# A fused decoder layer on one core: the second group's values and queries become filler of the second heads

## The chip, the cores and the metric

The kernel runs on one core of a Trainium2 chip. The metric is the time of one execution on the device in microseconds (us). Engines are named as in the profile: PE multiplies matrices (PEld loads its weights), DVE, ACT and POOL work on vectors, SP issues most transfers. Each engine works through its own queue in order; a semaphore wait at the head of a queue holds all that stands behind it.

## The reference

One decoder layer in float32 on x (512 tokens of 2048), with a norm at the end. After a first norm one projection gives the queries, keys and values of two groups of heads; both outputs are normed, joined and projected back, and a gated feed-forward part follows.

```
h = rmsnorm(x, ln_mix); proj = h @ w_in
sb_q, sb_k, sb_v, sw_q, sw_k, sw_v = split(proj)
sb_o = stick_breaking_attention(sb_q, sb_k, sb_v)              # 16 heads
sw_o = sliding_window_sink_attention(sw_q, sw_k, sw_v, sinks)  # 16 query heads, 4 key heads, window 128
x = x + concat(rmsnorm(sb_o), rmsnorm(sw_o)) @ w_out
h = rmsnorm(x, ln_ffn); x = x + (silu(h @ w_gate) * (h @ w_up)) @ w_down
return rmsnorm(x, ln_final)
```

A sliding-window head subtracts slope times distance from its scores, takes the maximum with a learned sink, exponentiates, divides by the sum and multiplies with the values.

## The kernel before

Every float32 operand is held as a high part and the rest (names ending in hi and lo), and a product is three matmuls: hi by hi, lo by hi, hi by lo. A weights' slab is 512 KB: a transfer on SP (`raw`, three tiles), a rounding to the high part on ACT (`whi`, L219, two tiles), the rest on DVE (`wlo`, L220, two tiles), then 24 matmuls of 128x512 or 48 of 128x256 on PE.

The stages, by the time in the profile: 0 to 59 us load and transposes of x, the split of the normed h (`h_make`), and the first projection (`add_kq`); here `left_sums` prepares sums of h for the following stage and `x_squares` squares x for the norm. To 140 the values of the first heads. To 431 the sixteen stick-breaking heads, "the first heads". To 458 the rest of their filler. From 459 to 603 the sliding-window heads, "the second heads": four groups of queries with four blocks of 128 tokens each, sixteen jobs. To about 730 the rest of the output projection, then the feed-forward part to the end at 2009.

**Filler.** An attention head alone would leave PE idle, so the projections around it are cut into slabs and put into `queue`. `step` issues one piece of the slab at its front; `pull(ns)` issues pieces worth so many nanoseconds, `drain(mark)` all up to a mark. `step` also loads the two slabs that come next and splits one. In the first heads the queue holds 32 slabs of queries and keys for the heads to come, the second heads' keys (swk), group 2's queries, and three of the four slabs of the second heads' values (swv); `sb_mark` ends it. In the second heads it holds the last slab of values, group 3's queries and the sixteen slabs of outA, which is the output projection of the first heads' half, column block by column block (`add_outA(c)`, c from 0 to 3). Behind them is outB.

`banks` of add_outA runs when a column block's first piece is issued:

```
x2[c] = v8.tile([P, NT, 512], F32, tag="v8", name="x2")
dma(out=x2[c], in_=x2d[:, c * 512:(c + 1) * 512].rearrange("(t p) c -> p t c", p=P))
```

`dma` keeps SP's transfers in the order in which the program issues them. `v8` is a pool of four tiles of 1 MB; a new tile takes one whose last reader is done. In the second heads v8 holds kst[0], qst[0] and qst[1] (the stacked keys of groups 0 and 1, the queries of groups 0 and 1) and x2; kst[1], qst[2] and qst[3] lie in another pool (`act8`).

**A job of the second heads** is spread over three rounds: scores (L1061, L1062) into a PSUM bank; on DVE the distance term (L1076) and the maximum (L1080); on ACT four exponentials (L1090); the scaling by the sum (L1102 ACT, L1104 DVE); transposes on PE (L1112); their high part on ACT (`phi`) and rest on DVE (`plo`, L1116); the product with the values (L1125, L1126). Four PSUM banks (`z`) serve scores, transposes and products. Between them stand four pulls of `SWFILL`/4.

The order on each engine is not the order of the code: a scheduler arranges the instructions, and only those issued through `pV`, `pA`, `pG`, `pT` and `dma` keep their program order.

Of the kernel before, what the change touches and what calls it, by code (L numbers as in the profile page):

```python
# [16 lines left out]
P = 128  # L17
# [4 lines left out]
HD = 64  # L22
# [15 lines left out]
def tile_hymba(ctx: ExitStack, tc: tile.TileContext, x, ln_mix, w_in, sb_norm, swa_norm,  # L38
# [27 lines left out]
    def act8(name, dt=F32R):  # L66
        return act.tile([P, 4, 512], dt, tag="a8", name=name, bufs=8)
# [10 lines left out]
    def po():  # L78
        return bank("o", 2)
# [14 lines left out]
    def tmp(dt=F32, name="t"):  # L94
        return phase[1].tile([P, 512], dt, tag="t", name=name, bufs=phase[2])
# [227 lines left out]
    def h_make(kt):  # L323
        pb = pz()
        for t in range(NT):
            pT.transpose(out=pb[:, t * P:(t + 1) * P], in_=xs[kt, t], identity=ident)
            warm({(0, 0): 1, (0, 1): 1, (0, 2): 3, (1, 3): 3}.get((kt, t), 0))
        if kt % 4 == 0:
            h8[0], h8[1] = act8("hhi"), act8("hlo")
        h_hi[kt], h_lo[kt] = h8[0][:, kt % 4, :], h8[1][:, kt % 4, :]  # L330
        split_scaled(pb, gcol[:, kt:kt + 1], h_hi[kt], h_lo[kt])
        if kt % 4 == 0:
            h8s.append((h8[0], h8[1]))
        if kt > 1:
            while vsum:
                vsum.pop(0)()
        left_sums(kt, pb)

    def left_sums(kt, pb):
        g, j, gc = kt // 8, kt % 4, gcol[:, kt:kt + 1]  # L340
        if kt % 8 == 0:
            vs = [v8.tile([P, 4, 512], F32, tag="v8", name="vs") for _ in range(2)]
            for k, p in enumerate("5736"):
                vleft[g, p] = vs[k // 2][:, :, (k % 2) * 256:(k % 2) * 256 + 256]
        s1, s3, s4, s2 = (vleft[g, p][:, j, :] for p in "5736")
        a, b = pb[:, 0:256], pb[:, 256:512]

        def stt(out, x, y, op):
            V.scalar_tensor_tensor(out=out, in0=x, scalar=gc, in1=y, op0=ALU.mult, op1=op)

        if kt % 8 < 4:
            pG.tensor_tensor(out=s1, in0=f(h_hi[kt])[:, 256:512], in1=f(h_lo[kt])[:, 256:512], op=ALU.add)
            vsum.append(lambda: stt(s3, a, s1, ALU.subtract))
        else:
            vsum.append(lambda: (stt(s1, b, s1, ALU.add), stt(s2, b, s3, ALU.subtract), stt(s4, a, s2, ALU.subtract)))

    def x_squares(c):
        for t in range(NT):
            xt = xs["c", c, t]
            A.activation(out=xt, in_=xt, func=AF.Square, accum_out=ss1[:, t, c:c + 1])  # L360

    def rstd1_make():
        sst = sm.tile([P, NT], F32, tag="sst", name="sst")
# [42 lines left out]
    def add_feat(w, cols, get_banks, done, hfn=hT):  # L406
        bk = {}

        def one(c, j, s):
            def go(hi, lo):  # L410
                k = s * 4 + j
                xh, xl = hfn(k)
                wh, wl = hi[:, j, c * P:(c + 1) * P], lo[:, j, c * P:(c + 1) * P]
                o = bk["b"][c]
                mm(o, lhsT=wh, rhs=xh, start=(k == 0), stop=False)  # L415
                mm(o, lhsT=wh, rhs=xl, start=False, stop=False)  # L416
                mm(o, lhsT=wl, rhs=xh, start=False, stop=(k == KT - 1))  # L417
                if k == KT - 1:
                    done(c, o)
                return 648.0  # L420
            return go

        for s in range(4):
            if s in (0, 3):
                mms = [one(c, j, s) for c in range(2) for j in range(4)]
            else:
                mms = [one(c, j, s) for j in range(4) for c in range(2)]
            queue.append(dict(srcs=[w[s * 512:(s + 1) * 512, c0:c0 + cn] for c0, cn in cols], a=4, b=256,
                              mms=mms, pre=(lambda: bk.update(b=get_banks())) if s == 0 else None,
                              post=None, prep=None, big=None))  # L430
# [117 lines left out]
    vst = [None] * NT  # L548
    swv = [None]
    kq = [None]  # L550
    KTS = ((), (2, 3), (4, 5), (6, 7), (8, 9, 10), (11, 12, 13), (14, 15), ())

    def add_kq():
        bk = {}

        def one(c, j, s):
            def go(hi, lo):
                k = s * 2 + j
                xh, xl = h_hi[k], h_lo[k]
                wh, wl = hi[:, j, c * P:(c + 1) * P], lo[:, j, c * P:(c + 1) * P]  # L560
                o = bk["b"][c]
                mm(o, lhsT=wh, rhs=xh, start=(k == 0), stop=False)
                mm(o, lhsT=wh, rhs=xl, start=False, stop=False)
                mm(o, lhsT=wl, rhs=xh, start=False, stop=(k == KT - 1))
                if k == KT - 1:
                    if c == 0:
                        kq[0] = const.tile([P, 4, 512], F32, tag="swv", name="kq")
                    if c % 2:
                        A.activation(out=kq[0][:, c, :], in_=o, func=AF.Copy)
                    else:  # L570
                        V.tensor_copy(out=kq[0][:, c, :], in_=o)
                return 648.0
            return go

        def prep(s):
            for kt in KTS[s]:
                h_make(kt)
            for c in {3: (0, 1), 5: (2,), 6: (3,)}.get(s, ()):
                x_squares(c)

        for s in range(8):
            order = [(c, j) for c in range(4) for j in range(2)] if s == 7 else [(c, j) for j in range(2) for c in range(4)]
            rows = slice(s * 256, (s + 1) * 256)
            queue.append(dict(srcs=[win[rows, C_SWQ:C_SWQ + 512]], a=2, b=512, big=None,
                              mms=[one(c, j, s) for c, j in order], post=None,
                              pre=(lambda: bk.update(b=four(1))) if s == 0 else None, prep=lambda s=s: prep(s)))
# [97 lines left out]
    def q_evac(pb, dst):  # L684
        V.scalar_tensor_tensor(out=dst, in0=pb, scalar=QSCALE, in1=rs1["b"], op0=ALU.mult, op1=ALU.mult)
# [13 lines left out]
    def stack_one(src, r0, st):  # L699

        s64 = src[r0:r0 + HD]
        r1 = HD - r0
        A.activation(out=st[r0:r0 + HD], in_=s64, func=AF.Copy)
        V.tensor_tensor(out=st[r1:r1 + HD], in0=s64, in1=f(st)[r0:r0 + HD], op=ALU.subtract)
# [50 lines left out]
        vof(n + 2, "to_hp")  # L755

    drain_to(5, 3)
    while vsum:
        vsum.pop(0)()
    x_squares(4)  # L760
    open_phase("vp", 1, reuse_waits="tile")
    for n in range(-6, 0):
# [43 lines left out]
    drain_to(11, 0)  # L806
    oA = [o8.tile([P, 4, 512], F32, tag="o8", name="oA") for _ in range(2)]
    kqs = ExitStack()
    kq2 = kqs.enter_context(tc.tile_pool(name="kq2", bufs=1, side="right", reuse_waits="tile")).tile([P, 4, 512], F32, name="kq2")
    add_feat(win, [(C_SWK, 256)], two_m, lambda c, pb: k_evac(pb, kq2[:, c, :]))  # L810
    add_feat(win, [(C_SWQ + 512, 256)], two_m, lambda c, pb: q_evac(pb, kq2[:, 2 + c, :]))
    add_swv()
    swv_end = len(queue)
    sb_mark = swv_end - 1
    z3 = {}
    for name in ("sh3", "sl3", "wh3", "wl3"):
        z3[name] = sbt(F32R, name, 256)
# [168 lines left out]
    def stack_keys(c):  # L986
        for e in range(2):
            stack_two(kq2[:, c, :], e * HD, kst[c][:, 2 * e, :], kst[c][:, 2 * e + 1, :])

    def stack_queries(g, src):  # L990
        for c in range(2):
            for e in range(2):
                stack_one(src[:, c, :], e * HD, qst[g][:, c * 2 + e, :])

    kst[0], qst[0], qst[1] = (v8.tile([P, 4, 512], F32R, tag="v8", name=n) for n in ("kst", "qst", "qst"))
    stack_keys(0)
    stack_queries(0, kq[0][:, 0:2, :])

    def add_swq3():
        def done(c, pb):  # L1000
            qf = tmp(name="qf")
            q_evac(pb, qf)
            for e in range(2):
                stack_one(qf, e * HD, qst[3][:, c * 2 + e, :])

        def tiles():
            kst[1], qst[2], qst[3] = act8("kst"), act8("qst"), act8("qst")

        n = len(queue)
        add_feat(win, [(C_SWQ + 768, 256)], lambda: [po(), po()], done)  # L1010
        queue[n + 1]["post"] = tiles

    add_swq3()
    swq3_end = len(queue)


    mixA = [None] * 10
# [117 lines left out]
    blks = {}  # L1135
    jobs = [(g, blk) for g in range(4) for blk in range(NT)]
    NJ = len(jobs)
    SWFILL = 5200.0 * 1.0
    at(swa_scores, 0)
    stack_queries(1, kq[0][:, 2:4, :])  # L1140
    for j in range(NJ + 2):
        at(swa_exp, j)
        pull(SWFILL / 4)
        at(swa_tr, j - 1)
        pull(SWFILL / 4)
        if j == 2:
            drain(swv_end)
        if j == 5:
            drain(swq3_end - 2)
            stack_keys(1)  # L1150
        if j == 6:
            stack_queries(2, kq2[:, 2:4, :])
        if j == 10:
            drain(swq3_end)
        at(swa_av, j - 2)
        pull(SWFILL / 4)
        at(swa_norm, j)
        at(swa_scores, j + 1)
        pull(SWFILL / 4)
# [692 lines left out]
```

## Time and profile before

| what | value |
|---|---|
| median of 3 runs | 2009.11 us (2008.97 to 2009.53) |
| the profiled execution | 2010.75 us, its span 2009.0 us |
| mean granted clock of PE | 0.997 |
| PE busy | 1992.6 us (99%) |
| DVE, ACT, POOL busy | 1498.7, 1503.0, 1106.1 us |

A timeline row reads: start, duration, engine, line, operation, output<-inputs, shape, count; in brackets the idle time of the engine just before and what ended it. A duration of a matmul overlaps the next one, so starts are compared. A row of the waits reads: engine, tile and line that waited, what for, us in total, times, longest. Rows of `wlo` at L220, of `whi` at L219 and of transfers at L100 are those of a helper; the tile tells which.

### The profile page before, as it was taken

What the parts mean: (1) busy time and instruction counts of PE and PEld (TensorE: products, weight loads), DVE (VectorE), ACT (ScalarE), POOL (GpSimd) and SP (SyncE); (2) the same over time, 40 slices, a digit from 0 to 9 for tenths busy, and PEclk for the clock granted to TensorE, in tenths of its full rate; (3) what the DMA queues carried; (4) which work ended last, traced back from release to release, by engine and by line L of the source; (5) the groups of instructions that cost most, each with busy time, mean ns of one, the idle gap of its engine ahead of it and who ended that gap; (6) DMA issues with size and microseconds to landing.
All of it is one profiled execution on the core that took longest, in us unless ns stands there. A gap on an engine that the chain in (4) does not pass through costs nothing.

```text
span 2009.0 us, 29374 instructions
## 1 busy us (share of the span) xinstructions
PE 1992.6 (99%) x10364; PEld 1700.1 (85%) x10364; DVE 1498.7 (75%) x2038; ACT 1503.0 (75%) x2063; POOL 1106.1 (55%) x597
## 2 busy tenths in 40 slices
PE   9999999999999999999999999999999999999998
PEld 8888888888788888888888888888888888888886
DVE  7677888868994777777777777777777867767767
ACT  6766777756773488777777777777777788888787
POOL 2742444420000076666766666576666778878883
PEclk9999999999999999999999999999999999999999
DMA  7312222222234445354444535445354743533523
GB/s 233 114 53 84 64 64 64 67 78 88 83 108 136 127 141 141 102 136 116 122 129 108 142 105 132 122 115 141 102 137 110 265 154 117 177 126 108 177 84 116
DMA packets 284323, 240.24 MB, mean 120 GB/s; under 512 B 11024, under 2 KB 233296, under 8 KB 281744
## 3 DMA queue, kind: packets, MB, share of 16 engines
q1 hardware_dynamic: 283504, 235.71, 39.5%
q8 instruction: 82, 1.34, 0.3%
q0 software_dynamic: 288, 1.32, 0.2%
q10 hardware_dynamic: 384, 1.34, 0.2%
q14 instruction: 65, 0.53, 0.1%
HBM read 218.40 MB, written 19.92 MB: 119 GB/s over the span
## 4 chain that ended last, share of the span: by engine, by line
PE 96%; DVE 2%; ACT 1%; issue 0%; DMA 0%; SPq 0%; POOL 0%; DVEq 0%; ACTq 0%
PE o L118 36%; PE m L118 30%; PE m L415 4%; PE m L416 4%; PE m L417 4%; PE m L384 2%; PE m L385 2%; PE m L383 2%; PE z L118 1%; PE o L385 1%; PE o L384 1%; PE o L383 1%; PE o L935 1%; PE z L851 1%; PE z L850 1%; PE z L914 0%
## 5 line engine op out<-in xcount | busy, mean ns | idle before, releaser
L118 DVE TENSOR_TENSOR wlo<-t,hp 128x1024 fp32r<-128x1024 f32 x247 | 301.1, 1219 | 184.3 <-PE o L118 113.0
L118 POOL TENSOR_TENSOR t<-raw,t 128x1024 f32<-128x1024 f32 x111 | 281.9, 2539 | 281.9 <-ACT hp L118 269.5
L118 ACT ACTIVATE whi<-t 128x1024 fp32r<-128x1024 f32 x247 | 262.0, 1061 | 125.8 <-PE o L118 76.0
L118 PE MATMUL o<-hca,whi 128*128 128x512 f32 x880 | 307.5, 391 | 0.0
L118 POOL TENSOR_TENSOR t<-raw,raw 128x1024 f32<-128x1024 f32 x114 | 294.5, 2586 | 21.3 <-issue 10.8
L118 DVE TENSOR_TENSOR wlo<-raw,hp 128x1024 fp32r<-128x1024 f32 x187 | 228.3, 1221 | 92.2 <-issue 52.1
L118 ACT ACTIVATE whi<-raw 128x1024 fp32r<-128x1024 f32 (+1 forms) x189 | 199.8, 1057 | 105.4 <-PE m L118 75.2
L118 ACT ACTIVATE hp<-t 128x1024 fp32r<-128x1024 f32 x247 | 249.1, 1009 | 2.5 <-POOL t L118 2.5
L118 PE MATMUL o<-hca,wlo 128*128 128x256 f32 x880 | 244.0, 280 | 0.0
L118 ACT ACTIVATE hp<-raw 128x1024 fp32r<-128x1024 f32 x191 | 192.8, 1009 | 3.8 <-DVE wlo L118 2.2
L118 PEld LDWEIGHTS o<-hca,whi 128*128 128x128 f32 x880 | 164.2, 187 | 35.8
L118 PE MATMUL m<-hca,whi 128*128 128x512 f32 x528 | 186.3, 392 | 1.1 <-DVE hca L118 1.1
L118 PEld LDWEIGHTS o<-hca,wlo 128*128 128x128 f32 x880 | 165.6, 189 | 0.4
L219 ACT ACTIVATE whi<-raw 128x1024 fp32r<-128x1024 f32 x87 | 91.7, 1054 | 85.7 <-PE o L385 33.1
L220 DVE TENSOR_TENSOR wlo<-raw,whi 128x1024 fp32r<-128x1024 f32 x87 | 109.0, 1253 | 59.8 <-ACT whi L219 59.2
L118 PE MATMUL m<-whi,dca 128*128 128x512 f32 x592 | 146.9, 389 | 0.0
L118 PE MATMUL o<-whi,dca 128*128 128x512 f32 x592 | 146.9, 389 | 0.0
L118 PE MATMUL m<-hca,wlo 128*128 128x256 f32 x528 | 146.3, 280 | 0.0
L415 PE MATMUL m<-hhi,whi 128*128 128x512 f32 x320 | 131.0, 409 | 0.0
L118 PEld LDWEIGHTS m<-whi,dca 128*128 128x128 f32 x592 | 111.1, 188 | 23.0
L118 PEld LDWEIGHTS o<-whi,dca 128*128 128x128 f32 x592 | 111.1, 188 | 23.1
L118 PE MATMUL m<-hcs,whi 128*128 128x512 f32 x352 | 125.9, 392 | 0.0
(386 smaller groups left out, 5266.9 us busy)
## 6 DMA issues: line engine op xcount, KB each, us to landing
raw<-in_w_gate_up_dram SPq DMA_DIRECT2D x348, 256.0 KB, 5.2
raw<-in_w_down_dram SPq DMA_DIRECT2D x68, 512.0 KB, 5.0
raw<-in_w_in_dram SPq DMA_DIRECT2D x35, 512.0 KB, 3.8
raw<-in_w_in_dram SPq DMA_DIRECT2D x66, 256.0 KB, 3.3
raw<-in_w_out_dram SPq DMA_DIRECT2D x32, 512.0 KB, 3.7
aT<-w SPq DMA_DIRECT2D x44, 256.0 KB, 3.5
xd<-aT SPq DMA_DIRECT2D x10, 1024.0 KB, 7.5
rx<-in_w_down_dram SPq DMA_DIRECT2D x20, 512.0 KB, 5.3
```

Source lines behind the costliest of these rows:

```text
L118: return lambda *a, **k: tc.keep_in_program_order(fn(*a, **k))
L219: A.activation(out=hi, in_=raw, func=AF.Copy)
L220: V.tensor_tensor(out=lo, in0=raw, in1=f(hi), op=ALU.subtract)
L383: mm(o, lhsT=lh[:, sl], rhs=hi[:, j, :], start=first, stop=False, skip_group_check=halves)
L384: mm(o, lhsT=lh[:, sl], rhs=lo[:, j, :], start=False, stop=False, skip_group_check=halves)
L385: mm(o, lhsT=ll[:, sl], rhs=hi[:, j, :], start=False, stop=(k == nslab * a - 1), skip_group_check=halves)
L415: mm(o, lhsT=wh, rhs=xh, start=(k == 0), stop=False)
L416: mm(o, lhsT=wh, rhs=xl, start=False, stop=False)
L417: mm(o, lhsT=wl, rhs=xh, start=False, stop=(k == KT - 1))
L850: mm(zb[:, 0:W], lhsT=kb, rhs=H.q1[:, c0:S], start=True, stop=False)
L851: mm(zb[:, 0:W], lhsT=kb, rhs=H.q2[:, c0:S], start=False, stop=True)
L935: mm(H.ob[:, c0:S], lhsT=vb, rhs=B.wl[:, 0:W], start=False, stop=(i == 0), skip_group_check=True)
```

## The change

There are two parts. In the x phase, the left sums and the squares of x are deferred by one piece (`defer(1, ...)`), so that they come behind the rounding of the next slab, and are issued so that the scheduler keeps them there. In the heads, the queue of the first heads ends behind swk (`sb_mark`); all four slabs of values and group 2's queries become filler of the second heads. Group 2 is projected into the `o` banks and stacked straight into its tile, as group 3 was (`add_swq(g)`); kst[1], qst[2] and qst[3] are tiles of v8. A `pull(8000)` stands ahead of the first scores, SWFILL is 6900 instead of 5200, the second keys are stacked at job 3, and each group's queries are drained just ahead of its first block. Line numbers behind the change differ by up to 4 from those before (scores L1059, transposes L1110, products L1123, slabs' matmuls L380 to L382 and L412 to L414).

```diff
--- before.py
+++ after.py
@@ -331,9 +331,6 @@
         split_scaled(pb, gcol[:, kt:kt + 1], h_hi[kt], h_lo[kt])
         if kt % 4 == 0:
             h8s.append((h8[0], h8[1]))
-        if kt > 1:
-            while vsum:
-                vsum.pop(0)()
         left_sums(kt, pb)
 
     def left_sums(kt, pb):
@@ -346,7 +343,7 @@
         a, b = pb[:, 0:256], pb[:, 256:512]
 
         def stt(out, x, y, op):
-            V.scalar_tensor_tensor(out=out, in0=x, scalar=gc, in1=y, op0=ALU.mult, op1=op)
+            pV.scalar_tensor_tensor(out=out, in0=x, scalar=gc, in1=y, op0=ALU.mult, op1=op)
 
         if kt % 8 < 4:
             pG.tensor_tensor(out=s1, in0=f(h_hi[kt])[:, 256:512], in1=f(h_lo[kt])[:, 256:512], op=ALU.add)
@@ -357,7 +354,7 @@
     def x_squares(c):
         for t in range(NT):
             xt = xs["c", c, t]
-            A.activation(out=xt, in_=xt, func=AF.Square, accum_out=ss1[:, t, c:c + 1])
+            pA.activation(out=xt, in_=xt, func=AF.Square, accum_out=ss1[:, t, c:c + 1])
 
     def rstd1_make():
         sst = sm.tile([P, NT], F32, tag="sst", name="sst")
@@ -548,6 +545,10 @@
     vst = [None] * NT
     swv = [None]
     kq = [None]
+    def flush():
+        while vsum:
+            vsum.pop(0)()
+
     KTS = ((), (2, 3), (4, 5), (6, 7), (8, 9, 10), (11, 12, 13), (14, 15), ())
 
     def add_kq():
@@ -575,8 +576,9 @@
         def prep(s):
             for kt in KTS[s]:
                 h_make(kt)
+            defer(1, flush)
             for c in {3: (0, 1), 5: (2,), 6: (3,)}.get(s, ()):
-                x_squares(c)
+                defer(1, lambda c=c: x_squares(c))
 
         for s in range(8):
             order = [(c, j) for c in range(4) for j in range(2)] if s == 7 else [(c, j) for j in range(2) for c in range(4)]
@@ -755,8 +757,6 @@
         vof(n + 2, "to_hp")
 
     drain_to(5, 3)
-    while vsum:
-        vsum.pop(0)()
     x_squares(4)
     open_phase("vp", 1, reuse_waits="tile")
     for n in range(-6, 0):
@@ -806,12 +806,11 @@
     drain_to(11, 0)
     oA = [o8.tile([P, 4, 512], F32, tag="o8", name="oA") for _ in range(2)]
     kqs = ExitStack()
-    kq2 = kqs.enter_context(tc.tile_pool(name="kq2", bufs=1, side="right", reuse_waits="tile")).tile([P, 4, 512], F32, name="kq2")
+    kq2 = kqs.enter_context(tc.tile_pool(name="kq2", bufs=1, side="right", reuse_waits="tile")).tile([P, 2, 512], F32, name="kq2")
     add_feat(win, [(C_SWK, 256)], two_m, lambda c, pb: k_evac(pb, kq2[:, c, :]))
-    add_feat(win, [(C_SWQ + 512, 256)], two_m, lambda c, pb: q_evac(pb, kq2[:, 2 + c, :]))
+    sb_mark = len(queue)
     add_swv()
     swv_end = len(queue)
-    sb_mark = swv_end - 1
     z3 = {}
     for name in ("sh3", "sl3", "wh3", "wl3"):
         z3[name] = sbt(F32R, name, 256)
@@ -992,26 +991,25 @@
             for e in range(2):
                 stack_one(src[:, c, :], e * HD, qst[g][:, c * 2 + e, :])
 
-    kst[0], qst[0], qst[1] = (v8.tile([P, 4, 512], F32R, tag="v8", name=n) for n in ("kst", "qst", "qst"))
-    stack_keys(0)
-    stack_queries(0, kq[0][:, 0:2, :])
-
-    def add_swq3():
+    smarks = [0] * 4
+
+    def add_swq(g):
         def done(c, pb):
+            if c == 0:
+                qst[g] = v8.tile([P, 4, 512], F32R, tag="v8", name="qst")
             qf = tmp(name="qf")
             q_evac(pb, qf)
             for e in range(2):
-                stack_one(qf, e * HD, qst[3][:, c * 2 + e, :])
-
-        def tiles():
-            kst[1], qst[2], qst[3] = act8("kst"), act8("qst"), act8("qst")
-
-        n = len(queue)
-        add_feat(win, [(C_SWQ + 768, 256)], lambda: [po(), po()], done)
-        queue[n + 1]["post"] = tiles
-
-    add_swq3()
-    swq3_end = len(queue)
+                stack_one(qf, e * HD, qst[g][:, c * 2 + e, :])
+
+        add_feat(win, [(C_SWQ + g * 256, 256)], (lambda: [po(), po()]) if g == 2 else two_m, done)
+        smarks[g] = len(queue)
+
+    kst[0], qst[0], qst[1], kst[1] = (v8.tile([P, 4, 512], F32R, tag="v8", name=n) for n in ("kst", "qst", "qst", "kst"))
+    stack_keys(0)
+    stack_queries(0, kq[0][:, 0:2, :])
+    for g in (2, 3):
+        add_swq(g)
 
 
     mixA = [None] * 10
@@ -1135,7 +1133,8 @@
     blks = {}
     jobs = [(g, blk) for g in range(4) for blk in range(NT)]
     NJ = len(jobs)
-    SWFILL = 5200.0 * 1.0
+    SWFILL = 6900.0
+    pull(8000.0)
     at(swa_scores, 0)
     stack_queries(1, kq[0][:, 2:4, :])
     for j in range(NJ + 2):
@@ -1145,13 +1144,10 @@
         pull(SWFILL / 4)
         if j == 2:
             drain(swv_end)
-        if j == 5:
-            drain(swq3_end - 2)
+        if j == 3:
             stack_keys(1)
-        if j == 6:
-            stack_queries(2, kq2[:, 2:4, :])
-        if j == 10:
-            drain(swq3_end)
+        if j + 1 < NJ and jobs[j + 1][1] == 0:
+            drain(smarks[jobs[j + 1][0]])
         at(swa_av, j - 2)
         pull(SWFILL / 4)
         at(swa_norm, j)
```

What the built order makes of it, at two places.

DVE where the second heads begin. `sst`, `rv`, `rt` and `rstdA` are the norm of the first heads' output, `s` a job's scores, `mx` their maximum. Before:

```order
490 L220 TENSOR_TENSOR wlo<-raw,whi 128x1024
491 L685 SCALAR_TENSOR_TENSOR kq_1425<-m,rbc_1350 128x512 x2
492 L220 TENSOR_TENSOR wlo<-raw,whi 128x1024 x3
493 L726 COPY sst<-o 128x4
494 L276 TENSOR_SCALAR rv<-sst 128x4
495 L976 CAST dist<-disti 128x256
496 L282 TENSOR_TENSOR rt<-rr 128x4
497 L283 TENSOR_TENSOR rt<-rt,rv 128x4
498 L284 TENSOR_SCALAR rt<-rt 128x4
499 L1076 SCALAR_TENSOR_TENSOR s<-dist,z 128x128
500 L286 TENSOR_TENSOR rstdA<-rr,rt 128x4
501 L1076 SCALAR_TENSOR_TENSOR s<-dist,z 128x128 x3
```

and with the change:

```order
483 L276 TENSOR_SCALAR rv<-sst 128x4
484 L706 TENSOR_TENSOR qst<-kq,qst 64x512
485 L282 TENSOR_TENSOR rt<-rr 128x4
486 L283 TENSOR_TENSOR rt<-rt,rv 128x4
487 L284 TENSOR_SCALAR rt<-rt 128x4
488 L286 TENSOR_TENSOR rstdA<-rr,rt 128x4
489 L1074 SCALAR_TENSOR_TENSOR s<-dist,z 128x128 x4
490 L1078 TENSOR_REDUCE mx<-s 128x2 x2
491 L1074 SCALAR_TENSOR_TENSOR s<-dist,z 128x256
492 L1080 TENSOR_TENSOR mx<-mx,sink 128x4
493 L1074 SCALAR_TENSOR_TENSOR s<-dist,z 128x256
494 L220 TENSOR_TENSOR wlo<-raw,whi 128x1024
```

The four low parts that stood ahead of `sst` are gone from there; the low part of the third slab of values now stands behind the norm (its copy of the sums and one cast stand just ahead of these rows), the first job's scores and maxima and two scores of the second job. On PE, 12 matmuls of the second slab and the scores of two jobs (16) stand between the norm's sums and the first matmul that reads it.

PE at the last scores of group 2 and the first of group 3 (qst_4938 and qst_5179 are group 3's queries, qst_4845 group 2's; numbers behind a name are buffers). Before, at group 3's first block:

```order
2803 L385 MATMUL o_5573<-whi_5691,mlo_5297 128x512
2804 L1061 MATMUL z_5816<-kst_4936,qst_4938 128x256
2805 L1062 MATMUL z_5816<-kst_4936,qst_4938 128x256
2806 L1061 MATMUL z_5816<-kst_4936,qst_4938 128x256
2807 L1062 MATMUL z_5816<-kst_4936,qst_4938 128x256
2808 L1061 MATMUL z_5821<-kst_4936,qst_4938 128x256
2809 L1062 MATMUL z_5821<-kst_4936,qst_4938 128x256
2810 L1061 MATMUL z_5821<-kst_4936,qst_4938 128x256
2811 L1062 MATMUL z_5821<-kst_4936,qst_4938 128x256
2812 L383 MATMUL o_5574<-whi_5691,mhi_5296 128x512
2813 L384 MATMUL o_5574<-wlo_5692,mhi_5296 128x512
2814 L385 MATMUL o_5574<-whi_5691,mlo_5297 128x512
```

and with the change, where group 2's last scores end:

```order
2767 L1059 MATMUL z_5736<-kst_4347,qst_4845 128x256
2768 L1060 MATMUL z_5736<-kst_4347,qst_4845 128x256
2769 L1110 MATMUL z_5782<-ident_85,s_5651 128x128 x2
2770 L1110 MATMUL z_5791<-ident_85,s_5651 128x128 x2
2771 L1110 MATMUL z_5782<-ident_85,s_5654 128x128 x2
2772 L1110 MATMUL z_5791<-ident_85,s_5654 128x128 x2
2773 L1123 MATMUL z_5809<-phi_5690,swv_4546 128x512
2774 L1124 MATMUL z_5809<-plo_5691,swv_4546 128x512
2775 L1123 MATMUL z_5809<-phi_5699,swv_4546 128x512
2776 L1124 MATMUL z_5809<-plo_5700,swv_4546 128x512
2777 L1059 MATMUL z_5841<-kst_4347,qst_5179 128x256
2778 L1060 MATMUL z_5841<-kst_4347,qst_5179 128x256
```

Six more scores stand behind these, and then the slab whi_5675. Before, filler stood on both sides of a job's scores; now 28 rows of scores, transposes and products follow one another without filler. A like stretch of 38 rows ends with the transposes and products that follow the last scores of group 3. On SP the load of x2[1] stands just ahead of the load of the slab whi_5675 is made from, as it did before.

## Prediction

> **What bounds the kernel now.** I read the page first, then the waits of PE, then the rows around the longest one.
>
> ```profile
> PE 1992.6 (99%) x10364; PEld 1700.1 (85%) x10364; DVE 1498.7 (75%) x2038; ACT 1503.0 (75%) x2063; POOL 1106.1 (55%) x597
> ```
>
> PE is the bound: 16.4 of the span's 2009.0 us are idle, and the change neither adds nor removes a matmul. So the time moves only by PE's waits and by its clock. The waits in the stretches that the change touches:
>
> ```profile
> PE m L384 <- DVE wlo L220: 1.9, 1, 1.9
> PE m L564 <- DVE wlo L220: 0.7, 1, 0.7
> PE o L935 <- DVE l L925: 0.7, 2, 0.4
> PE z L1112 <- ACT s L1102: 0.6, 1, 0.6
> PE z L1112 <- DVE s L1104: 0.4, 1, 0.4
> ```
>
> L564 is in the x phase, L935 at the end of the first heads, the other three lie in the second heads: 4.3 us in all. The longest costs more than itself. Timeline of PE, then the windows (columns: PE, PEld, DVE, ACT, POOL, granted clock, DMA share, GB/s):
>
> ```profile
> 527.12 0.65 PE L384 MATMUL m<-wlo,mhi 128*128 128x512 f32 x1 [1.85 <-DVE wlo L220]
> ...
> 527.00:528.00 1.00, 0.88 (x3) 0.69 (x4) 0.96 (x5) 0.41 (x3) 0.00 (x0) 0.65 0.00 0
> 529.00:530.00 1.00, 1.00 (x4) 0.81 (x3) 1.00 (x6) 0.30 (x1) 0.00 (x0) 0.50 0.96 369
> 530.00:531.00 1.00, 1.00 (x6) 0.70 (x6) 0.78 (x3) 0.00 (x0) 0.00 (x0) 0.64 0.15 55
> ```
>
> After 1.85 us without work the clock stands at one half from 527.1 to about 530.5, so some 3.4 us do the work of 1.7: another 1.7 us. Everything that these stretches could give back is 0.7 + 0.7 + 2.9 + 1.7 = 6.0 us, 0.3% of the time. A measurement of this kernel can tell 0.2% (4 us) from no change.
>
> **The x phase.** The left sums and the squares go behind the next slab's rounding.
>
> ```profile
> 12.14 1.41 DVE L272 SCALAR_TENSOR_TENSOR hlo<-z,gcol,hhi 128x512 fp32r<-128x512 f32 x2 [1.39 <-ACT hhi L271]
> 13.74 0.49 DVE L349 SCALAR_TENSOR_TENSOR vs<-z,gcol,vs 128x256 f32<-128x256 f32 x1 [0.19 <-POOL vs L118]
> 14.14 1.34 DVE L220 TENSOR_TENSOR wlo<-raw,whi 128x1024 fp32r<-128x1024 f32 x1
> ```
>
> The low part ends at 15.48 and PE waits for it. Without the left sum ahead, and the 0.19 us that this waited for POOL, it would follow the split that ends at 13.55; in the new order it even comes before that split. The wait goes: **-0.7 us**. The sums land in later slabs' time, where no wait stands on this page.
>
> **The end of the first heads.** Their filler loses the second group's queries and the values, so less is left there. Between the sums of the last head's third key block and its last product stand 39 filler matmuls of 128x512 before, and 56 of 128x256 in the new order.
>
> ```profile
> 523.44 0.39 PE L1126 MATMUL z<-plo,swv 128*128 128x512 f32 x1
> 523.67 0.28 PE L1061 MATMUL z<-kst,qst 128*128 128x256 f32 x1
> 523.78 0.28 PE L1062 MATMUL z<-kst,qst 128*128 128x256 f32 x1
> ...
> 430.73 0.50 PE L935 MATMUL o<-l,vst 128*128 128x512 f32 x1 [0.37 <-DVE l L925]
> 436.26 1.29 POOL L718 TENSOR_TENSOR sqA<-sqA,oc 128x512 f32<-128x512 f32 x1 [15.33 <-DVE qst L704]
> ```
>
> At 0.23 and 0.12 us from start to start these are 9.0 and 6.7 us, against a chain of exponentials that already overran its cover by 0.7: up to 2.3 more. Some of the old cover was not needed, so I take 1.3. Behind it stand 28 matmuls (3.4 us) and then the norm's sums, which need POOL's sqA; before, that ended (437.55) 6.3 us after the last product (431.23), but partly behind four query stacks and a low part on DVE, which the new order thins. I take 0.9 of a possible 3. Together **+2.2 us** (0 to 5).
>
> **The entry into the second heads.** DVE stands so before (its first score also waits for the norm's factors):
>
> ```profile
> 458.56 0.95 PE L723 MATMUL o<-ones,sqA 128*128 128x2 f32 x8
> ...
> 459.55 0.16 DVE L726 COPY sst<-o 128x4 f32<-128x4 f32 x1 [4.23 <-PE o L723]
> 461.31 0.29 DVE L1076 SCALAR_TENSOR_TENSOR s<-dist,z 128x128 f32<-128x128 f32 x1
> 462.18 0.74 DVE L1080 TENSOR_REDUCE mx<-s 128x2 f32<-128x256 f32 x2
> 463.70 1.22 DVE L220 TENSOR_TENSOR wlo<-raw,whi 128x1024 fp32r<-128x1024 f32 x1
> ```
>
> Before, the values' slabs were split long ahead. Now the low part of the third one stands behind this whole row of DVE. Counted from the sums' matmuls: copy at 1.0; 1.8 to the first score, and a query stack of 0.7 of which 0.2 hides, 3.3; four scores 0.9, two maxima 0.7, two larger scores 0.7, the low part 1.2: 6.8. PE does in that time the sums (0.8), 12 filler matmuls (1.4), 16 score matmuls (1.9) and two of the new slab (0.2) and stands at 4.5: 2.3 us of waiting, more than the 1.85 that halved the clock: **+4.0 us** (0.5 to 5).
>
> By the Trainium skill (TensorE: Matmul & The Clock Gate, Part 1: The HAM clock gate) the clock falls only after an idle window of some 3.4 us, and this gap would cost no clock; 1.7 us would leave the sum. The rows above, where 1.85 us sufficed, differ from it, and the measurement decides.
>
> **Fourth job.** Here the stacks of group 2's queries and of the second keys now meet on DVE.
>
> ```profile
> 516.85 2.09 DVE L704 TENSOR_TENSOR qst<-kq,qst 64x512 fp32r<-64x512 f32 x3
> ...
> 465.00:600.00 135.00, 132.17 (x689) 110.96 (x688) 126.27 (x313) 106.40 (x269) 7.47 (x5) 0.99 0.31 98
> ```
>
> DVE has little slack in this stage (126 of 135 us busy). Four query stacks and two key stacks at 0.7, four casts at some 0.4 and two evacuations at 0.7 now come between one job's score and its scaling: 7.3 us beside a job's own 7.2. PE has 48 fillers there (11.0 us) and 20 rows of other jobs (2.8), 13.8 against 14.5. I take **+0.9 us** (0 to 1.3). The three old waits and their clock go: **-4.6 us**.
>
> **What the loads of x wait for.** This is what decides. outA's column c begins with the load of x2[c] into a tile of v8, on SP, and the next weights' slab stands behind it in SP's queue. Before, v8 held kst[0], qst[0], qst[1], and the later keys and queries lay in act8; x2[1] and x2[2] took the tiles of the first two groups, long free. Now kst[1], qst[2] and qst[3] live in v8: x2[0] waits for the last scores of group 1, x2[1] for those of group 2, x2[2] for the very last scores. The transfers before:
>
> ```profile
> raw<-in_w_out_dram SPq DMA_DIRECT2D x16, 512.0 KB, 3.7
> x<-in_x_dram SPq DMA_DIRECT2D x4, 1024.0 KB, 6.7
> ...
> xd<-aT SPq DMA_DIRECT2D x10, 1024.0 KB, 7.5
> ...
> 512.41 0.46 SPq L100 DMA_DIRECT2D x<-in_x_dram  x1
> 527.13 22.70 SPq L100 DMA_DIRECT2D raw<-in_w_out_dram  x4
> ...
> 584.00:585.00 1.00, 1.00 (x6) 0.81 (x5) 0.99 (x4) 1.00 (x6) 0.00 (x0) 1.00 1.02 279
> 587.00:588.00 1.00, 1.00 (x10) 1.00 (x9) 1.00 (x2) 0.64 (x2) 0.00 (x0) 1.00 1.01 393
> 590.00:591.00 1.00, 1.00 (x6) 0.83 (x5) 0.99 (x4) 1.00 (x6) 0.00 (x0) 1.00 0.93 260
> 591.00:592.00 1.00, 1.00 (x7) 0.81 (x6) 0.99 (x3) 1.00 (x6) 0.00 (x0) 1.00 0.54 209
> ```
>
> One x load fills all DMA engines (share 1.0) and lands after 6.7 us; a slab alone takes them 1.5 us. A slab issued right behind it lands 6.7 + 1.5 = 8.2 us after the x load's issue, at the least 0.5 + 3.7 = 4.2 if the two interleave. I take 8.2, since the share leaves no room beside it. Then comes whi on ACT:
>
> ```profile
> 521.80 1.11 PE L1112 MATMUL z<-ident,s 128*128 128x128 f32 x8 [0.38 <-DVE s L1104]
> 522.66 0.47 PE L1125 MATMUL z<-phi,swv 128*128 128x512 f32 x1
> ...
> 522.00 1.04 ACT L219 ACTIVATE whi<-raw 128x1024 fp32r<-128x1024 f32 x1
> 525.24 0.51 ACT L1090 ACTIVATE s<-s,nmx 128x256 f32<-128x256 f32 x1 [0.47 <-DVE nmx L1084]
> ```
>
> So 9.25 us pass between the last scores of a group and the next filler matmul. Prices of what PE has meanwhile: eight transposes 0.86 (521.80 to 522.66), four products 1.0, eight scores 0.94 (0.12 each), a filler 0.23.
>
> x2[0]: behind the scores stand 36 to 37 filler rows still loaded, and one set of transposes and products, 8.7 us; 0.6 left, and 0.3 for the low part: **+0.9 us**.
>
> x2[1]: the last loaded filler stands ahead of the scores. Behind them only transposes, products and the next eight scores, 2.8 us: 6.45 idle. The low part takes 1.2, the four matmuls ahead of it 0.9: 0.3 more. The clock falls again, 1.7 less the 0.2 that the wait covers: 6.8 + 1.5 = **+8.3 us**. Even with the slab there early, whi stands on ACT behind group 2's last job:
>
> ```profile
> 511.88 1.41 DVE L1076 SCALAR_TENSOR_TENSOR s<-dist,z 128x256 f32<-128x256 f32 x4
> 513.21 1.27 DVE L1080 TENSOR_REDUCE mx<-s 128x2 f32<-128x512 f32 x2
> ```
>
> DVE begins it 0.7 late, then the scores 1.35, the maxima 1.25 and two rests of phi (0.6 each), the exponentials 2.0 and whi itself 1.0: 7.5, so 4.7 idle and 0.3.
>
> x2[2]: filler ends one job earlier still, so the last scores themselves wait 1.2 us for a bank that DVE frees. Then 1.86 us of work in 9.25, 7.4 idle, 0.3 for the low part, 1.5 for the clock: **+10.4 us**.
>
> The end gives nothing: 22 filler matmuls (5.0 us) now stand behind the last product instead of 81, as long as the chain of sums that they cover.
>
> **Sum.** -0.7 + 2.2 + 4.0 + 0.9 - 4.6 + 0.9 + 8.3 + 10.4 = +21.4 us. The profiled run took 2010.75, 1.6 over the median 2009.1 and 1.75 over its span; the difference is put on the median: **2030.5 us**.
>
> **Rivals.** *The tiles come free in time* (not slower; faster). If x2[1] and x2[2] are loaded early, as the row at 512.41 was 15 us ahead of the next slab, and the values cover the entry, all of 6.0 us returns: 2003. For it: before, no slab of this stage was late. Against: the four v8 tiles are counted above. It decides from the point at which 41 fillers (9.25 / 0.23) are loaded behind the scores. 7%.
>
> *Enough filler left, but the entry stays*: without the three last terms +1.8, 2011, no change. The same count speaks against it: 37, 0 and 0 rows. 7%.
>
> *Landing beside the x load*: 4.2 instead of 8.2 takes 0.9, 1.8 and 0.7 away, and if the clock holds as well, 4.7: 2022. Within the forecast's range, as is *the half clock lasts through the gaps*, where the 2.8 and 4.7 us of attention work double: 2038.
>
> **How the numbers follow.** The forecast with its bounds 86%, of which 2 above and 3 below the range. The low end takes the early landing, the clock held and no loss in the first heads (21.4 - 3.4 - 4.7 - 2.2 = 11.1, 2020); the high end the doubled work and an x load that lands after 7.5, as xd does (+2.4, and 5.5 for the doubled work at the gaps' ends): 2039. Range 2020 to 2039. Faster 7%, no change 7%, slower 86%.
>
> **What would show it.** In the new trace: two waits of PE of 5 to 8 us for whi or wlo of an outA slab (L380, L381), each ending about 9 us after an x load was issued and with a slab issued within 1 us behind it; that slab's landing at 7 to 8 us; a granted clock near 0.5 behind each; a wait of 2 us at the first values' slab in the second heads; L564 gone. Wrong would be an x load issued well ahead of its group's last scores, or PE at work while it is on its way.

## The result

The changed kernel takes 2029.14 us (median of 4 runs, 2027.9 to 2030.19) against 2009.27 before (2008.97 to 2009.53). The ratio is 1.0099, with a 95% interval of 1.0081 to 1.0116: slower by 1%. The profiled execution took 2027.9 us and has a span of 2026.2, 17.2 us more than that of before.

The page, the waits of PE, the timeline of SP and the windows around the first gap, of the changed kernel (columns of a window: length; PE, PEld, DVE, ACT, POOL; granted clock, DMA share, GB/s):

```profile
span 2026.2 us, 29383 instructions
PE 1997.1 (99%) x10364; PEld 1703.6 (84%) x10364; DVE 1499.1 (74%) x2038; ACT 1504.0 (74%) x2063; POOL 1104.2 (54%) x597
```

```profile
PE z L1110 <- DVE s L1102: 4.9, 2, 4.2
PE m L380 <- ACT whi L219: 4.1, 2, 3.7
PE m L381 <- DVE wlo L220: 2.4, 1, 2.4
PE z L1059 <- DVE plo L1114: 1.8, 2, 1.0
PE o L725 <- POOL sqA L720: 1.4, 1, 1.4
...
PE z L910 <- DVE e L872: 0.8, 1, 0.8
PE z L913 <- DVE l L878: 0.6, 1, 0.6
```

```profile
514.50 0.37 SPq L100 DMA_DIRECT2D x<-in_x_dram  x1
514.97 9.09 SPq L100 DMA_DIRECT2D raw<-in_w_out_dram  x4
553.42 0.37 SPq L100 DMA_DIRECT2D x<-in_x_dram  x1
553.88 9.18 SPq L100 DMA_DIRECT2D raw<-in_w_out_dram  x4
593.89 0.37 SPq L100 DMA_DIRECT2D x<-in_x_dram  x1
594.35 9.32 SPq L100 DMA_DIRECT2D raw<-in_w_out_dram  x4
```

```profile
553.06 0.28 PE L1060 MATMUL z<-kst,qst 128*128 128x256 f32 x1
553.18 1.37 PE L1110 MATMUL z<-ident,s 128*128 128x128 f32 x8
...
557.01 0.39 PE L1059 MATMUL z<-kst,qst 128*128 128x256 f32 x1 [0.79 <-DVE plo L1114]
...
561.46 1.06 PE L380 MATMUL m<-whi,mhi 128*128 128x512 f32 x2 [3.71 <-ACT whi L219]
```

```profile
557.00:559.00 2.00, 0.74 (x4) 0.53 (x4) 1.96 (x9) 1.26 (x5) 0.00 (x0) 1.00 1.02 365
559.00:561.00 2.00, 0.00 (x0) 0.00 (x0) 1.58 (x8) 1.46 (x5) 0.00 (x0) 1.00 0.99 370
561.00:563.00 2.00, 1.54 (x4) 1.25 (x5) 1.52 (x4) 2.00 (x6) 0.00 (x0) 0.67 0.56 216
563.00:565.00 2.00, 2.00 (x6) 1.51 (x6) 1.70 (x4) 1.89 (x9) 0.00 (x0) 0.50 0.49 133
```

Idle time of PE grew from 16.4 to 29.1 us, and PE's busy time by 4.5 us although it does the same matmuls, in part because more of them ran at half clock. The waits in the old list for a low part at 527, for the scaled scores and for the x phase's low part are gone. Of the new ones, those of 0.8 and 0.6 for e and l and that for sqA belong to the end of the first heads, that of 2.4 for a low part to the entry, and one of 0.8 for s to the fourth job. The rest, from 553 us on, are what the SP rows explain. The last scores of group 2 are issued at 553.06, the load of x2[1] at 553.42, and the slab that PE needs next at 553.88. PE works off transposes, products and one more set of scores and then waits until 561.46. For 3.4 us behind it the clock is at one half. The same comes again at 593.89, for the last group, but there the clock falls while PE still waits, at 595.8, and stays at one half until 602.6.

### The profile page after: what moved, and what is told of

It reads as the page before. It is cut to its first block, busy times and chain, and to the rows that moved or that the text cites. A ratio compares the mean times of both kernels' runs of the same rounds, so it can differ in the third digit from the quotient of the medians.

```text
span 2026.2 us, 29383 instructions
## 1 busy us (share of the span) xinstructions
PE 1997.1 (99%) x10364; PEld 1703.6 (84%) x10364; DVE 1499.1 (74%) x2038; ACT 1504.0 (74%) x2063; POOL 1104.2 (54%) x597
## 4 chain that ended last, share of the span: by engine, by line
PE 74%; DVE 2%; ACT 1%; DMA 1%; issue 0%; POOL 0%; DVEq 0%; ACTq 0%; POOLq 0%
PE o L118 34%; PE m L118 28%; PE m L381 2%; PE m L380 2%; PE m L382 2%; PE o L380 1%; PE o L381 1%; PE o L382 1%; PE z L118 1%; DMA raw<-in_w_out_dram 1%; PE z L1110 0%; PE o L414 0%; PE o L412 0%; PE o L413 0%; PE z L1184 0%
## 5 line engine op out<-in xcount | busy, mean ns | idle before, releaser
L412 PE MATMUL m<-hhi,whi 128*128 128x512 f32 x320 | 131.3, 410 | 0.0
```

## The experiments

Seven kernels ran. The theory was that the loads of x block SP's queue, since their tiles of v8 are held by kst[1], qst[2] and qst[3]. Its rival was that the moved filler itself overloads DVE in the second heads.

**The tiles alone**, in the kernel before, no filler moved:

```diff
-            kst[1], qst[2], qst[3] = act8("kst"), act8("qst"), act8("qst")
+            kst[1], qst[2], qst[3] = (v8.tile([P, 4, 512], F32R, tag="v8", name=n) for n in ("kst", "qst", "qst"))
```

> The kernel before, with nothing changed but the place of kst[1], qst[2] and qst[3]: tiles of v8 instead of act8. No filler is moved. x2[1] now waits for the last scores of group 2 and x2[2] for those of the last job. If the blocked loads are the cause: two waits of PE of 3 to 5 us and 5 to 7 us in the second heads, each behind an x load that is issued right at those scores, each with some 3.4 us at half clock after it; 2019 to 2026 us, about +13. If the cause is the moved filler (values and queries that overload DVE in the second heads), this kernel has none of it and stays at 2009 within 2.

Measured: 2025.57 us against 2009.77, ratio 1.0075 (1.006 to 1.009). Timelines of SP and of PE:

```profile
551.73 0.37 SPq L100 DMA_DIRECT2D x<-in_x_dram  x1
589.82 0.37 SPq L100 DMA_DIRECT2D x<-in_x_dram  x1
...
555.43 1.94 PE L1112 MATMUL z<-ident,s 128*128 128x128 f32 x8 [3.08 <-DVE s L1104]
560.47 0.73 PE L383 MATMUL m<-whi,mhi 128*128 128x512 f32 x2 [0.68 <-ACT whi L219]
597.96 1.22 PE L383 MATMUL m<-whi,mhi 128*128 128x512 f32 x2 [4.45 <-ACT whi L219]
```

Both gaps are there, with none of the moved filler: one line that only names another pool costs 15.8 us, 80% as much as the whole change. (A wait of 1.86 for whi at 522.30 and two small ones are in the place of the old stall there.)

**The tiles out of the way**, in the changed kernel:

```diff
-    kst[0], qst[0], qst[1], kst[1] = (v8.tile([P, 4, 512], F32R, tag="v8", name=n) for n in ("kst", "qst", "qst", "kst"))
+    kst[0], qst[0], qst[1] = (v8.tile([P, 4, 512], F32R, tag="v8", name=n) for n in ("kst", "qst", "qst"))
+    kst[1] = swp.tile([P, 4, 512], F32R, name="kst", bufs=1)
...
-    swp = open_phase("swp", 15)
+    swp = open_phase("swp", 13)
```

> The changed kernel, with kst[1] in a tile of its own (and 13 instead of 15 temporary tiles in the second heads, to make room), so that each x2 finds a v8 tile one group earlier; the order of SP's queue stays as changed. The blocked loads as cause: no x load is issued later than a group's scores that are one group back, no gap, 2011 to 2015. The moved filler as cause, or the queue's order by itself: 2025 or more.

Measured: 2013.87 us, ratio 1.0017 (1.0008 to 1.0026). Waits of PE:

```profile
PE m L381 <- DVE wlo L220: 3.0, 2, 2.7
PE o L725 <- POOL sqA L720: 1.4, 1, 1.4
...
PE z L910 <- DVE e L872: 0.9, 1, 0.9
PE z L913 <- DVE l L878: 0.6, 1, 0.6
```

Between 445 and 620 us one wait of 0.33 is left, although DVE has the same work as in the changed kernel: DVE was not the bound, the late slabs were. The 15 us that this gives back are three quarters of the loss; the rest are the entry and the end of the first heads, as listed. (In this trace 6.8 us at half clock begin in the entry's wait.)

**The order of SP's queue**, in the changed kernel, tiles as changed:

```diff
-            dma(out=x2[c], in_=x2d[:, c * 512:(c + 1) * 512].rearrange("(t p) c -> p t c", p=P))
+            defer(12, lambda: dma(out=x2[c], in_=x2d[:, c * 512:(c + 1) * 512].rearrange("(t p) c -> p t c", p=P)))
```

> The changed kernel, with the load of x2[c] issued 12 pieces after its column's start, so that two slabs' loads go ahead of it in SP's queue; tiles and filler stay as changed. If the blocked loads are the cause, the two gaps of 6.7 and 9.7 us (waits and half clock) vanish and only the entry (2.4), the norm's sums (1.4), the fourth job (0.8) and the ends of the first heads (1.6) remain: 2011 to 2015. If DVE is overloaded by the moved filler or by the larger pulls, the waits for s, plo and whi stay: 2025 or more.

Measured: 2018.87 us, ratio 1.0043 (1.0026 to 1.0059), above what was expected. The gap at 553 is gone. The other one stayed, as the timelines of SP and PE show:

```profile
593.93 0.37 SPq L100 DMA_DIRECT2D x<-in_x_dram  x1
594.39 9.20 SPq L100 DMA_DIRECT2D raw<-in_w_out_dram  x4
...
601.99 1.02 PE L380 MATMUL m<-whi,mhi 128*128 128x512 f32 x2 [3.54 <-ACT whi L219]
```

With filler between them, the very last scores stand later behind column 2's start than the 12 pieces by which its x load was put off. The expectation had taken that distance from the order in which filler is missing. So the queue's order is a cure only where the wait is shorter than what was put ahead.

**The x phase alone**, in the kernel before (the sums' emptying in `h_make` and behind `drain_to(5, 3)` goes as in the change):

```diff
-            V.scalar_tensor_tensor(out=out, in0=x, scalar=gc, in1=y, op0=ALU.mult, op1=op)
+            pV.scalar_tensor_tensor(out=out, in0=x, scalar=gc, in1=y, op0=ALU.mult, op1=op)
...
+            defer(1, flush)
...
-                x_squares(c)
+                defer(1, lambda c=c: x_squares(c))
```

> The kernel before with only the x phase's part of the change: left sums and squares behind the next slab's rounding. The wait at L564 of 0.74 us goes: 2008.4 to 2008.9, the same as before to the measurement; as in the changed kernel's trace a wait of 0.3 for a load of x may take part of it back. A rival, that the later sums delay the value passes: 2009.5 or more, with a new wait there.

Measured: 2008.83 us against 2009.77, ratio 0.9994 (0.9984 to 1.0003): no difference that can be told. In its trace the wait at L564 is gone and none is new. Its span is 1.9 us shorter than that of before, but not for this wait alone: the old wait at 527, here 1.87 us, was not followed by half clock (last section).

**The mark back**, on top of the kernel with the keys elsewhere:

```diff
-    sb_mark = len(queue)
     add_swv()
     swv_end = len(queue)
+    sb_mark = swv_end - 1
```

> As the run with the keys elsewhere (2013.9), and three of the four slabs of values are back in the first heads' queue (the mark that ends it stands one slab before the values' end, as before). If the price that is left there comes from the end of the first heads and the entry, their waits (1.7 in the last sums, 1.45 for sqA, 2.65 for the third slab's low part, and some 1.7 of half clock) go: 2006 to 2008. A rival: the pull of 8 us ahead of the first scores makes the entry's gap, whatever the mark; then a wait of 2 us or more stays at the first slab behind the first scores: 2010 to 2012.

Measured: 2013.97 us against 2010.55, ratio 1.0023 (1.0014 to 1.0032). The entry's gap is down to 0.7 and 0.3, now for values (swv), and the waits at the end of the first heads to 0.9 and 1.0. But the time is no shorter: the expectation was wrong, and the wait of 2 us or more that its rival put behind the first scores is not there either. The waits of PE, and the timelines of SP and PE:

```profile
PE m L380 <- ACT whi L219: 2.0, 2, 1.7
PE o L725 <- POOL sqB L720: 1.6, 1, 1.6
```

```profile
514.59 0.37 SPq L100 DMA_DIRECT2D x<-in_x_dram  x1
515.07 9.16 SPq L100 DMA_DIRECT2D raw<-in_w_out_dram  x4
...
522.63 0.73 PE L380 MATMUL m<-whi,mhi 128*128 128x512 f32 x2 [1.66 <-ACT whi L219]
```

The queue is three slabs shorter and is pulled as hard as before, so column 0 starts earlier, and now x2[0] meets the last scores of group 1: the same gap at a third place. At the end filler is short too, and the norm's sums wait 1.6.

**The mark back, and the pulls with it**:

```diff
-    SWFILL = 6900.0
-    pull(8000.0)
+    SWFILL = 6500.0
```

> The same, without the pull of 8 us ahead of the first scores and with pulls of 6500 instead of 6900 a job, which is what the shorter queue is worth. If the gaps come from where filler is short and not from how much is pulled: 2004 to 2007, faster than the kernel before by 2 to 5 us, which are its three waits and the half clock in the second heads and the wait of the x phase. The rival of the last run: clearly faster than that run, by 2 us or more.

Measured: 2007.17 us (2006.74 to 2007.6) against 2010.55, ratio 0.9984 (0.9974 to 0.9993): faster than the kernel before, by 3.4 us. Between 445 and 620 us PE waits for nothing that the profile shows, and the clock of the run is 0.999. So moved filler can give something, once the tiles, the mark and the pulls fit. It is a smaller change, though: three of the four slabs of values are back in the first heads, and of the moved filler group 2's queries are left. Which of the two numbers (the pull or SWFILL) matters was not tried.

**The changed kernel once more**:

> The changed kernel once more, with nothing edited, for the clock behind its gaps. In its first profile the wait of 2.37 us at the entry was followed by full clock, in the run with the keys elsewhere 2.65 us by 0.5, and with x behind the slabs the clock fell to 0.5 ahead of a wait of 1.25 us. If the length of a gap decides, the entry is again followed by full clock and the time is 2027.9 within 0.5; if it depends on where a gap falls in time, the clock there can be 0.5 now, and the time is then 1 to 2 us longer.

Measured: 2027.65 us. The entry's wait is again 2.4 us and again followed by full clock. That fits a rule by length as well as one by place; the last section tells them apart with the other traces.

## Why the prediction was right

It gave 2030.5 us and the right cause; the median is 2029.14. Its terms were less exact than that. Step by step, in the trace:

| step | predicted | in the trace |
|---|---|---|
| x phase | -0.7 | wait of 0.74 gone, one of 0.33 for a load of x new; the first heads start 0.4 earlier: -0.4 |
| end of the first heads and sqA | +2.2 | 0.8 + 0.6 + 0.2 + 1.45 instead of 0.74: +2.3 |
| entry | +2.3, and 1.7 of clock | +2.4, clock full: +2.4 |
| fourth job | +0.9 | +0.8 |
| old waits of the second heads | -4.6 | none left: -4.6 |
| x2[0] | +0.9 | 0 |
| x2[1] | +8.3 | +7.2 |
| x2[2] | +10.4 | +8.2 |
| end | 0 | +0.4 (the sums of the second norm wait for sqB) |
| sum | +21.4 | +16.3, and 17.2 between the spans |

No row accounts for the 0.9 us between the two last numbers. The two gaps in the right column are worked out from starts. Behind the last scores of group 2 (553.18) PE had 2.8 us of work, so filler could have gone on at 556.0; it did at 561.46, and 1.7 us of clock follow: 7.2. Ahead of the last gap the scores of group 3's third block end at 590.15; transposes, products and the last job's pieces are 4.1 us at full clock, 594.3. Filler came at 602.07, and lost another 0.45 to the clock: 8.2.

```profile
590.15 1.04 PE L1110 MATMUL z<-ident,s 128*128 128x128 f32 x8
...
593.12 0.39 PE L1059 MATMUL z<-kst,qst 128*128 128x256 f32 x1 [1.00 <-DVE plo L1114]
598.02 1.94 PE L1110 MATMUL z<-ident,s 128*128 128x128 f32 x8 [4.16 <-DVE s L1102]
602.07 0.97 PE L380 MATMUL m<-whi,mhi 128*128 128x512 f32 x2 [0.40 <-ACT whi L219]
```

The wrong size was in the step "a slab issued right behind it lands 6.7 + 1.5 = 8.2 us after the x load's issue". Here is ACT's row of that slab, in the changed kernel:

```profile
560.35 1.06 ACT L219 ACTIVATE whi<-raw 128x1024 fp32r<-128x1024 f32 x1 [0.54 <-DMA raw<-in_w_out_dram]
```

It landed just ahead of 560.35, 6.9 us after the x load was issued at 553.42. The x load itself took 5.3, not 6.7. The step read a DMA share of 1.0 as a full rate. The windows it quoted moved 279 and 393 GB/s at the same share, and in this gap 365 to 370 GB/s went through on average: there was room beside a lone x load after all. So filler comes 8.0 us after the x load's issue (553.42 to 561.46) instead of 9.25. It did so in every gap that ended with a slab: 8.2 (593.89 to 602.07), 8.1 in the kernel with x behind the slabs (593.93 to 601.99), 8.0 with the mark back (514.59 to 522.63), 8.1 in the second gap with the tiles alone (589.82 to 597.96). With 8.1 the 8.7 us of work behind x2[0] cover it, which is why that term is 0: the scores end at 514.24, PE comes to the new slab at 522.91, and its whi was ready at 522.40. (That step's 36 to 37 filler rows do not fit its own sum: at 0.23 us, with the transposes and products, they would be some 10 us. In the trace 30 rows stand there, and 8.7 us is right.) The other two terms lose 1.2 each.

The other error was the clock. At the entry it did not fall, which takes away 1.7 us; whether it falls hangs on where the gap lies (last section), and the prediction had no means to tell. At x2[2] it fell during the wait and rose again at 602.6, so that it cost filler 0.45 us instead of 1.5. To this extent the rival of half clock through the gap came true: the last transposes and products ran at one half, but ended before the slab was there. Two smaller sums do not come out as written: PE's four terms at the entry add up to 4.3 and not 4.5, and the fourth job's 14.5 less 13.8 is 0.7, not 0.9.

The signs that the prediction named were there in kind and not all in size. The slabs let filler go on 8.0 and 8.2 us after the x loads, not 9.25, and the slab landed after 6.9 us instead of 7 to 8. The waits for whi are 3.7 and 0.4 us instead of 5 to 8: the rest of each gap stands in the list as waits of the attention jobs for `plo` and `s`.

That the number was closer than its terms is chance: the sum was made on a profiled execution that took 1.6 us more than its median, and the changed kernel's profiled one took 1.2 less than its own. Of the 19.9 us between the medians the two traces show 17.2. No trace shows the rest. (The mean granted clock was 0.995 in the changed kernel's three other executions and 0.996 in the profiled one, so some of it can be half clock.)

Of the rivals, *the tiles come free in time* and *enough filler left* are refuted by the SP rows. *Landing beside the x load* was partly true, as told.

## What to carry to other kernels

When a buffer moves to another pool, look up who takes its place next, what that one's write waits for, and on which queue: here a load issued at 553.42, whose tile was first read at 571.07, stood at the head of the queue and held the weights that PE needed at once. A small change of places can so cost more than the waits it was made for, and the built order together with the tiles' last readers tells it before a run. A queue of filler, its end mark and the amounts pulled from it belong together; to change one of them moves every later meeting of filler and buffers.

## What the runs showed of the hardware

How long a gap is does not tell whether the clock falls behind it. In all nine traces the changes of the granted clock lie whole multiples of 3.413 us apart. In the changed kernel half clock begins at 561.67 and at 595.80, which is ten times 3.413; with the tiles alone it begins at 524.29, 555.01 and 595.97, nine and twelve times. Within the work it lasts 3.41 or 6.83 us each time. So the clock is set anew on a grid of stretches of 3.413 us, and the rows show what a stretch has to hold: enough idle time of PE within it. Windows laid on the grid (same columns as above; the idle time is the length less the busy time of PE, the next number). They are two each of the kernel before, of the x phase alone, of the changed kernel, of the keys elsewhere and of x behind the slabs:

```profile
523.89:527.30 3.41, 1.56 (x11) 1.17 (x10) 3.41 (x8) 2.92 (x11) 0.00 (x0) 1.00 0.00 0
527.30:530.71 3.41, 3.41 (x9) 2.53 (x10) 3.37 (x14) 1.02 (x4) 0.00 (x0) 0.50 0.57 154
...
522.31:525.73 3.42, 2.54 (x16) 1.99 (x14) 3.42 (x9) 2.91 (x7) 0.00 (x0) 1.00 0.02 5
525.73:529.14 3.41, 2.42 (x13) 2.00 (x14) 3.37 (x12) 2.19 (x9) 0.00 (x0) 1.00 0.29 95
...
435.37:438.79 3.42, 2.24 (x19) 2.03 (x17) 3.29 (x15) 1.79 (x2) 0.62 (x1) 1.00 0.00 0
438.79:442.20 3.41, 2.23 (x18) 2.23 (x19) 3.40 (x8) 1.75 (x9) 0.00 (x0) 1.00 0.32 87
...
435.77:439.19 3.42, 1.46 (x13) 1.25 (x11) 3.39 (x14) 1.51 (x2) 0.00 (x0) 1.00 0.00 0
439.19:442.60 3.41, 2.72 (x12) 2.72 (x13) 3.41 (x9) 1.12 (x6) 0.00 (x0) 0.50 0.46 135
...
431.59:435.01 3.42, 2.35 (x20) 2.35 (x21) 2.48 (x5) 0.34 (x3) 1.76 (x3) 1.00 0.00 0
435.01:438.42 3.41, 3.41 (x18) 3.41 (x18) 3.00 (x12) 1.97 (x3) 0.74 (x1) 0.50 0.00 0
```

In the kernel before, the wait of 1.85 us lay in one stretch, and half clock followed. With the x phase alone the same wait, 1.87 us, was cut by the grid into 0.88 and 0.99, and the clock stayed full. The entry's 2.37 us of the changed kernel were cut in halves of 1.18: full clock. Of the 2.65 us with the keys elsewhere 1.96 lay in one stretch: half clock. Between 420 and 650 us of the nine traces, all ten stretches at full clock with 1.85 us or more of idle PE were followed by half clock. Of those with 1.60 or less only one was, the last pair above: 1.07 us, the part of the wait of 1.44 for sqA that lies in it. That stretch also holds the eight short matmuls of the norm's sums (128x2, 0.9 us); a stretch of the changed kernel with 0.89 us and the same matmuls kept full clock, so why it fell here is open. No run moved a gap along the grid on purpose, and between 1.60 and 1.85 us no trace of this stage has a stretch.

The Trainium skill (TensorE: Matmul & The Clock Gate, Part 1: The HAM clock gate) says that the activity window is free-running and that the point of transition depends on where in the window the first matmul lands. The grid agrees with a free-running window. Its figure of an idle window of about 3.4 us fits the length of the stretches, but not the idle time that sufficed: 1.85 us in one stretch were enough.
